# One YOCO hybrid decoder step: where the sampled sequences' new SSD states and the bias tables are made

## The chip, the cores and the metric

The kernel runs as one program on one core of a Trainium2 chip. A core has a matrix engine (TensorE, "PE" in the profile, with its weight loads listed apart as "PEld"), a vector engine (VectorE, "DVE"), an activation engine (ScalarE, "ACT"), a general engine (GpSimd, "POOL") and an engine that here only issues DMAs (SyncE, "SP"). Each works through its own list of instructions in a fixed order, and they wait for each other through semaphores. The metric is the device time of one execution in microseconds. A change is judged by the ratio of the two kernels' times in interleaved rounds on the same chip.

## What is computed

The reference is one inference step of a small two-layer decoder, for one prompt of 512 tokens and eight sampled sequences of four tokens each (544 tokens in all, width 1024). Layer one is a Mamba-2 mixer, layer two a dilated window attention; both share their weights between the prompt and the samples. Cut to what matters here:

```python
u = rmsnorm(h, g_norm) @ w_in              # 5120 columns: gate z, x, B, C (and dt)
act = silu(causal_conv(xBC))               # width 4, from state_conv for the samples
# chunked scan; for a sampled sequence there is one chunk of 4 tokens:
y      = y_diag + C @ s_in * exp(a_cs)     # reads the old state s_in
s_new  = exp(a_last) * s_in + B^T (decay_in * dt * x)      # an output, read by nothing else
h = h + rmsnorm(y * silu(z)) @ w_out       # 8 tiles of 128 columns, 16 blocks deep
kv = rmsnorm(h) @ w_kv                     # 16 tiles: 8 of values, 8 of keys
bias = rel_bias[bucket(distance)]          # per head and dilation group
... dilated attention over kv and a cache with those biases, then @ w_o, final norm
```

For the eight samples the state is 8 x 32 heads x 64 x 128 floats (8.4 MB); the old states come in as `s0`, the new ones leave as `ssmS`. The bias tables depend on the weights alone.

## The kernel before

All products are made in pairs of rounded halves: a weight tile `wraw` is split by ScalarE into a high part (`whi`, L199) and by VectorE into a low part (`wlo`, L200), activations likewise, and three matmuls (high x high, high x low, low x high) replace one. A tile of columns is done as two halves of tokens, `pa` (256) and `pb` (288). The matrix engine's instructions keep the order in which the code issues them; the other engines' orders are made by a planner that takes the earliest instruction of the program that its model holds ready, with some work raised by `high_priority` (the weight splits above all).

Buffers come from pools with a fixed number of slots for each tag. Those that matter here are `slab` (`half`, 13 slots of 128x4x544 floats, used through the whole kernel), `ss` (`pss`, five banks of PSUM), `wraw` (three raw weight tiles), and in the second stage the tag `hb` (two slots).

Four stages follow one another:

- **Stage A** (to about 368 us of the profile): the 40 tiles of `w_in` run through the matrix engine as a filler (`filler_a`), and a list of 24 units is woven in: for each of four groups `g`, four prompt chunks (`ssm_chunk`) and two quads of sampled sequences (`ssm_quad`, `q` = 0, 1; four sequences each). A quad loads its old states in two halves (`s_t`, L685), multiplies them with the output weights (`yos`, L699), splits B (`bt`, L700) and the weighted inputs (`xr`, L714) into rows of high and low parts, lets GpSimd multiply the old states in place with their decays (L723) and then, for each sequence, makes `up` on the matrix engine, adds it to the state on VectorE (L744) and stores two sequences at a time from ScalarE's DMA queue (L746). A state buffer can be loaded again only when its store has landed.
- **The out stage** (about 368 to 473 us): eight tiles of `w_out`, each 16 blocks deep, so 96 matmuls. `h1_tile` adds the residual and prepares the next activations. One step of the generator `bias_tables` runs after each tile.
- **The kv stage** (about 473 to 580 us): 16 tiles, values first, each 48 matmuls. Two steps of `bias_tables` run in each tile until it is through: 7 steps of `bvp` products, then 12 of `bs` products, each copied out by VectorE (L901, L913) and stored to DRAM. The **quarters** `bq` are the attention layer's normalized activations, their sums and differences, split into high and low parts (L1021 to L1035); they need only `h1` and the norm `rs_h`, which the second kv tile provides, and the planner puts them beside the kv tiles. They take seven slots of the slab.
- **The attention stage** (from 580 us): first products `pa<-bq`, then attention, output projection and final norm.

Of the kernel before, what the change touches and what calls it, by code (L numbers as in the profile page):

```python
# [12 lines left out]
F32 = mybir.dt.float32  # L13
# [111 lines left out]
def tile_yoco_step(  # L125
# [86 lines left out]
    def hi_lo_rows(out, src, c, rows=128):  # L212
        nc.scalar.activation(out, src, AF.Copy, scale=hls[0:rows, c + 1:c + 2])
        nc.vector.scalar_tensor_tensor(out, src, hls[0:rows, c:c + 1], f32(out), op0=ALU.mult, op1=ALU.add)
# [69 lines left out]
    sed = dram.tile([2, NH, 32], F32, name="sed")  # L284
    vnd = dram.tile([NB, TS, ATH, 128], F32, name="vnd")
    kvd = dram.tile([ATH, 128, T + SEQ], F32, name="kvd")

# [205 lines left out]
    def spread_decays():  # L493
        dx = pss("dx")
        mm(dx[:, 0:384], ones, dgs.rearrange("p a b -> p (a b)"), start=True, stop=True)
        dv = dx[:, 0:384].rearrange("p (r j h) -> p r j h", r=3, j=4)
        nc.scalar.copy(dec[:, 0:4], dv[:, 0])
        nc.scalar.copy(dec[:, 4:12].rearrange("p (j r) h -> p r j h", r=2), dv[:, 1:3])

    def tok_transposes():  # L500
# [162 lines left out]
    def ssm_quad(g, q):  # L663
# [34 lines left out]
        for j in range(4):  # L698
            mm(yo[32 * j:32 * j + 32, :], cp[:, q, j, :], s_t[j // 2][:, j % 2, :], start=True, stop=True)  # L699
        bt = wk.tile([128, 128], F32R, name="btr", bufs=1)  # L700
        hi_lo_rows(bt, cbp[:, 128:256], 0)
        cbm = wk.tile([128, 16], F32, name="cbs")
# [9 lines left out]
        with tc.high_priority():  # L712
            nc.vector.tensor_tensor(xdd, xph, bc(tok[:, 4 + q, 2, hs], HP), op=ALU.mult)
        xr = wk.tile([128, 8, HP], F32R, name="xr", bufs=1)  # L714
        hi_lo_rows(xr, xdd, 2)
        ms = wk.tile([128, 8, 16], F32, name="ms")
# [3 lines left out]
        nc.vector.tensor_tensor(ms, ms, cbm[:, None, :].to_broadcast([128, 8, 16]), op=ALU.mult)  # L720
        for j in range(4):
            sv = s_t[j // 2][:, j % 2, :].rearrange("p (a b) -> p a b", b=HP)
            nc.gpsimd.tensor_tensor(sv, sv, bc(dec[:, 4 + 4 * q + j, hs], HP), op=ALU.mult)  # L723
        yield
# [13 lines left out]

        def update(j):
            up = pss("up", (128, 8, HP))  # L740
            mm(up.rearrange("p a b -> p (a b)"), bt[32 * j:32 * j + 32, :],
               xr[32 * j:32 * j + 32].rearrange("p a b -> p (a b)"), start=True, stop=True)
            sv = s_t[j // 2][:, j % 2, :].rearrange("p (a b) -> p a b", b=HP)
            nc.vector.tensor_tensor(sv, up, sv, op=ALU.add)  # L744
            if j % 2:
                nc.scalar.dma_start(ssmS[g, :, 4 * q + j - 1:4 * q + j + 1, :], s_t[j // 2])  # L746

        for j in range(3):
            update(j)
        yield  # L750
        update(3)

# [91 lines left out]
    def h1_tile(m, pa, pb):  # L844
# [16 lines left out]
        (nc.gpsimd if m < KD - 1 else nc.vector).tensor_tensor(hss, hss, sq, op=ALU.add)  # L861

    def load_out(m):
        return [load_w(w_out[m, :, 0:8, :]), load_w(w_out[m, :, 8:16, :])]

    def bias_tables():
        rl = wk.tile([66, 384], F32, name="rl", tag="tv", bufs=2)
        relt = wk.tile([66, 384], F32R, name="relt", bufs=1)
        for i in range(2):
# [8 lines left out]
        def fetch(q):  # L878
            oh = wk.tile([66, 2 * SK], F32R, name="oh", tag="tb", bufs=2)
            if q < 2:  # L880
                oh = oh[:, 0:VN // 2]
                hot(oh, ohp[:, q * (VN // 2):(q + 1) * (VN // 2)])
            elif q < 8:
                oh = oh.rearrange("p (a b) -> p a b", a=2)
                hot(oh, ohs[:, 2 * q - 4:2 * q - 2, :])
            return oh
# [3 lines left out]
        for q in range(8):  # L890
            oh, nxt = nxt, fetch(q + 1)
            if q < 2:
                ov = wk.tile([128, VN // 2], F32, name="ov", tag="tv", bufs=2)
                c = 0
# [11 lines left out]
                continue  # L906
            bsr = wk.tile([128, 2, SK], F32, name="bsr", tag="tv", bufs=2)
            g, t = divmod(2 * q - 4, TS)
# [12 lines left out]
    for m in range(KD):  # L921
        w = nxt
        pa, pb = pj("pa"), pj("pb")
        if m == 0:
            full(pa, w, v_h, v_l, 0, HA, 0, 12)
            full(pb, w, v_h, v_l, HA, T, 0, 12)
            full(pa, w, v_h, v_l, 0, HA, 12, 15)
            full(pb, w, v_h, v_l, HA, T, 12, 15)
            ms_add(ms, ssq, inv_i, True, True)
            full(pa, w, v_h, v_l, 0, HA, 15)  # L930
            full(pb, w, v_h, v_l, HA, T, 15)
            nxt = load_out(1)
            prev = pa, pb
            continue
# [7 lines left out]
        if m + 1 < KD:  # L942
            nxt = load_out(m + 1)
        full(pb, w, v_h, v_l, HA, T)
        h1_tile(m, pa, pb)
        next(tables, 0)

# [29 lines left out]
    for i, (f, h, wi) in enumerate(order):  # L977
        w = [nxt]
        pa, pb = pj("pa"), pj("pb")
        if i == 0:  # L980
# [6 lines left out]
            full(pb, w, h_h, h_l, HA, T, 7)  # L987
            prev = pa, pb
            continue
        if i == 1:  # L990
# [12 lines left out]
        next(prev, 0)  # L1003
        next(tables, 0)
        full(pb, w, h_h, h_l, HA, T, 4)
# [3 lines left out]
        next(prev)  # L1009
        next(tables, 0)  # L1010
        if i == 8:
# [594 lines left out]
```

## Time and profile before

| what | value |
|---|---|
| median of 3 runs | 957.39 us (952.74 to 958.02) |
| the profiled execution, its own time | 955.35 us |
| its span, first to last instruction | 953.6 us |
| VectorE, ScalarE, GpSimd busy | 685.5, 477.6, 201.9 us |
| granted TensorE clock over the span | 0.983 |
| DMA, mean over the span | 177 GB/s |

The span is what the views of the profile divide up; 1.75 us of the execution lie outside it. A busy share of an engine says little by itself: the matrix engine's busy time counts a matmul from its start to the modelled end of its pipeline, so that neighbouring matmuls overlap. What one costs is read from the distance between starts.

### The profile page before, as it was taken

The page shows a single profiled execution, that of the slowest core. Times are in us where ns is not written, and L with a number is a line of the kernel's source. Part 1 is how long each engine was busy: PE and PEld are TensorE (multiplying, and loading weights), DVE is VectorE, ACT ScalarE, POOL GpSimd, SP SyncE. Part 2 cuts the span into 40 slices and gives each one's busy share as a digit, 9 for nine tenths or more (in the row PEclk, how much of TensorE's full clock was granted, in tenths as well). Part 3 has the DMA queues.
Part 4 walks back from the last instruction along what each step waited for, and adds up shares of the span by engine and source line. Part 5 has one row for each costly group of instructions (what it writes and reads, how often), then busy time and mean ns, then how long its engine had stood idle before and what let it go on. Part 6 is the DMA issues. An engine that isn't in the chain of part 4 may idle for free.

```text
span 953.6 us, 21793 instructions
## 1 busy us (share of the span) xinstructions
PE 924.2 (97%) x8645; PEld 850.3 (89%) x8645; DVE 685.5 (72%) x1435; ACT 477.6 (50%) x1057; POOL 201.9 (21%) x295
## 2 busy tenths in 40 slices
PE   7999999899999998999999999999999999999896
PEld 5999888888888888999999999988888888879896
DVE  5688998998999888555488446866667767758532
ACT  5557754755655654322254213555545555566442
POOL 3232544734634732101101000000000000000121
PEclk9999999899999999999999999999999999999898
DMA  7252355254465433536286555766877767855311
GB/s 253 91 138 93 100 200 187 84 191 151 153 206 174 172 113 111 155 101 216 97 275 215 186 176 182 261 217 214 271 236 251 258 236 215 292 194 193 113 47 48
DMA packets 75934, 168.49 MB, mean 177 GB/s; under 512 B 19446, under 2 KB 37192, under 8 KB 75320
## 3 DMA queue, kind: packets, MB, share of 16 engines
q1 hardware_dynamic: 71880, 154.91, 49.5%
q10 hardware_dynamic: 2880, 9.44, 2.5%
q0 software_dynamic: 1072, 2.74, 1.1%
q8 instruction: 68, 1.11, 0.5%
q14 instruction: 34, 0.28, 0.1%
HBM read 141.14 MB, written 25.93 MB: 175 GB/s over the span
## 4 chain that ended last, share of the span: by engine, by line
PE 87%; DVE 6%; DMA 3%; ACT 1%; POOL 1%; issue 1%; SPq 0%; DVEq 0%; ACTq 0%
PE pa L143 34%; PE pb L143 30%; PE sp L143 3%; PE so L143 3%; PE pv L143 2%; PE s L143 2%; DMA kc<-ck 1%; PE yd L143 1%; PE csp L143 1%; PE yo L143 1%; PE ptp L146 1%; PE xp L146 1%; PE w L146 1%; DVE co L529 1%; PE yos L143 1%
## 5 line engine op out<-in xcount | busy, mean ns | idle before, releaser
L199 ACT ACTIVATE whi<-wraw 128x1024 fp32r<-128x1024 f32 x72 | 76.1, 1056 | 101.5 <-PE pb L143 68.9
L200 DVE TENSOR_TENSOR wlo<-wraw,whi 128x1024 fp32r<-128x1024 f32 x71 | 90.0, 1268 | 48.1 <-ACT whi L199 47.9
L143 PE MATMUL pa<-bq,whi 128*128 128x272 f32 x512 | 103.2, 297 | 0.0
L143 PE MATMUL pa<-xh,whi 128*128 128x256 f32 (+1 forms) x320 | 92.9, 294 | 3.3 <-ACT xh L365 3.3
L143 PE MATMUL pb<-xh,whi 128*128 128x288 f32 (+1 forms) x304 | 90.4, 299 | 3.9 <-ACT cb L331 3.9
L143 PE MATMUL pb<-xl,whi 128*128 128x288 f32 (+1 forms) x304 | 91.2, 302 | 0.9 <-DVE xl L368 0.8
L143 PE MATMUL pa<-xl,whi 128*128 128x256 f32 (+1 forms) x320 | 90.7, 287 | 1.1 <-DVE xl L368 1.1
L143 PE MATMUL pb<-xh,wlo 128*128 128x288 f32 (+1 forms) x304 | 87.4, 299 | 0.0
L143 PE MATMUL pa<-xh,wlo 128*128 128x256 f32 (+1 forms) x320 | 85.0, 283 | 0.0
L143 PEld LDWEIGHTS pa<-bq,whi 128*128 128x128 f32 x512 | 81.9, 190 | 0.9
L143 PE MATMUL pb<-bq,whi 128*128 128x272 f32 x384 | 78.4, 298 | 1.0 <-DVE qpad L1091 0.7
L143 PE MATMUL pa<-bq,wlo 128*128 128x272 f32 x256 | 74.3, 290 | 0.0
L529 DVE SCALAR_TENSOR_TENSOR co<-cb,cvp,co 128x568 f32<-128x568 f32 x72 | 66.1, 919 | 1.1 <-ACT co L527 0.2
L143 PEld LDWEIGHTS pa<-xh,whi 128*128 128x128 f32 x320 | 60.8, 190 | 6.4 <-ACT xh L365 4.0
L143 PEld LDWEIGHTS pa<-xl,whi 128*128 128x128 f32 x320 | 60.6, 189 | 3.5 <-DVE xl L368 1.6
L143 PEld LDWEIGHTS pb<-xl,whi 128*128 128x128 f32 x304 | 57.8, 190 | 6.4 <-issue 4.4
L143 PEld LDWEIGHTS pb<-bq,whi 128*128 128x128 f32 x384 | 61.4, 190 | 2.3 <-DVE qpad L1091 1.4
L143 PEld LDWEIGHTS pb<-xh,whi 128*128 128x128 f32 x304 | 58.0, 191 | 5.0 <-ACT cb L331 4.1
L1333 POOL COPY lse<-mxs 128x1 f32<-128x1 f32 x16 | 4.1, 258 | 265.5 <-DVE mxs L1331 265.5
L143 PEld LDWEIGHTS pa<-xh,wlo 128*128 128x128 f32 x320 | 58.0, 188 | 1.3 <-issue 0.9
L143 PEld LDWEIGHTS pb<-xh,wlo 128*128 128x128 f32 x304 | 56.6, 190 | 2.2 <-issue 2.2
L1158 ACT ACTIVATE whi<-wraw 128x512 fp32r<-128x512 f32 x64 | 40.1, 626 | 35.9 <-PE pb L143 14.8
(378 smaller groups left out, 2788.0 us busy)
## 6 DMA issues: line engine op xcount, KB each, us to landing
wraw<-w_in SPq DMA_DIRECT2D x40, 512.0 KB
kc<-ck SPq DMA_DIRECT2D x32, 640.0 KB
vc<-cv SPq DMA_DIRECT2D x32, 640.0 KB
wraw<-wb SPq DMA_DIRECT2D x32, 512.0 KB
s<-s SPq DMA_DIRECT2D x16, 512.0 KB
m<-aed SPq DMA_DIRECT2D x16, 512.0 KB
ssmS<-s ACTq DMA_DIRECT2D x16, 512.0 KB
wraw<-w_out SPq DMA_DIRECT2D x16, 512.0 KB
```

Of the source, the lines that this page charges most:

```text
L143: pin(nc.tensor.matmul(*a, **k))
L146: pin(nc.tensor.transpose(*a))
L199: a = nc.scalar.activation(hi, raw, AF.Copy)
L200: b = lo_eng.tensor_tensor(lo, raw, f32(hi), op=ALU.subtract)
L529: nc.vector.scalar_tensor_tensor(o, cb[:, k:k + n], cvp[:, ti, k:k + 1], o, op0=ALU.mult, op1=ALU.add)
L1158: nc.scalar.activation(hi, src[p][j], AF.Copy)
L1333: nc.gpsimd.tensor_copy(lse[:, i16:i16 + 1], mx[:, 2:3])
```

## The change

In stage A a quad no longer makes its new states. It still loads the old ones and multiplies them with `cp`, but then only copies B (`bt`) and writes it and the weighted inputs (`xdd`) to a DRAM tensor `sxd`; the decays of all samples are written once to `dcd`. The new states are made in the out and kv stages by three functions. `state_load(k)` loads the four old states of quad `k` again (1 MB), with `sxd` and `dcd`; `state_prep(k)` multiplies them with the decays on GpSimd and makes the rows of high and low parts; `state_fin(k)` makes the four `up` products, adds them and stores, now from GpSimd's DMA queue. `state_step` is called twice per out tile (once in the first) and once per kv tile; quad `k` is loaded at step 3k, prepared at step 3k+2, finished at step 3k+4. So quad 0 is finished with out tile 2 and quad 7 at step 25, after kv tile 10. `bias_tables` leaves the out stage: it starts in kv tile 0, skips tile 1 and takes two steps per tile from tile 2 on, which puts its last product in tile 11. Its buffers come from the slab, as those of the states take its former room.

```diff
+    sxd = dram.tile([NG, 2, 128, 640], F32, name="sxd")
+    dcd = dram.tile([128, NG, 8, 8], F32, name="dcd")
...
+        for g in range(NG):
+            dma(dcd[:, g], dec[:, 4:12, 8 * g:8 * g + 8])
...
-        bt = wk.tile([128, 128], F32R, name="btr", bufs=1)
-        hi_lo_rows(bt, cbp[:, 128:256], 0)
+        bt = wk.tile([128, 128], F32, name="bts", bufs=2)
+        nc.scalar.copy(bt, cbp[:, 128:256])
+        dma(sxd[g, q, :, 512:640], bt)
...
-        xr = wk.tile([128, 8, HP], F32R, name="xr", bufs=1)
-        hi_lo_rows(xr, xdd, 2)
+        dma(sxd[g, q, :, 0:512], xdd.rearrange("p a b -> p (a b)"))
...
-        for j in range(4):
-            sv = s_t[j // 2][:, j % 2, :].rearrange("p (a b) -> p a b", b=HP)
-            nc.gpsimd.tensor_tensor(sv, sv, bc(dec[:, 4 + 4 * q + j, hs], HP), op=ALU.mult)
...
-        def update(j):
-            up = pss("up", (128, 8, HP))
-            mm(up.rearrange("p a b -> p (a b)"), bt[32 * j:32 * j + 32, :],
-               xr[32 * j:32 * j + 32].rearrange("p a b -> p (a b)"), start=True, stop=True)
-            sv = s_t[j // 2][:, j % 2, :].rearrange("p (a b) -> p a b", b=HP)
-            nc.vector.tensor_tensor(sv, up, sv, op=ALU.add)
-            if j % 2:
-                nc.scalar.dma_start(ssmS[g, :, 4 * q + j - 1:4 * q + j + 1, :], s_t[j // 2])
-
-        for j in range(3):
-            update(j)
         yield
-        update(3)
...
+    def state_load(k):
+        g, q = divmod(k, 2)
+        s_ = wk.tile([128, 4, 512], F32, name="sx", bufs=2)
+        dma(s_, s0[g, :, 4 * q:4 * q + 4, :])
+        sx = wk.tile([128, 640], F32, name="sxx", bufs=2)
+        dma(sx, sxd[g, q])
+        dq = wk.tile([128, 4, 8], F32, name="dq", bufs=2)
+        dma(dq, dcd[:, g, 4 * q:4 * q + 4])
+        st_q[k] = [s_, sx, dq]
+
+    def state_prep(k):
+        s_, sx, dq = st_q[k]
+        for j in range(4):
+            sv = s_[:, j, :].rearrange("p (a b) -> p a b", b=HP)
+            nc.gpsimd.tensor_tensor(sv, sv, bc(dq[:, j], HP), op=ALU.mult)
+        bt = wk.tile([128, 128], F32R, name="btr", bufs=1)
+        hi_lo_rows(bt, sx[:, 512:640], 0)
+        xr = wk.tile([128, T], F32R, name="xr", tag="hb", bufs=2)[:, 0:512]
+        hi_lo_rows(xr, sx[:, 0:512], 2)
+        st_q[k] += [bt, xr]
+
+    def state_fin(k):
+        g, q = divmod(k, 2)
+        s_, _, _, bt, xr = st_q.pop(k)
+        for j in range(4):
+            up = pss("up")
+            mm(up, bt[32 * j:32 * j + 32, :], xr[32 * j:32 * j + 32, :], start=True, stop=True)
+            nc.vector.tensor_tensor(s_[:, j, :], up, s_[:, j, :], op=ALU.add)
+            if j % 2:
+                nc.gpsimd.dma_start(ssmS[g, :, 4 * q + j - 1:4 * q + j + 1, :], s_[:, j - 1:j + 1, :])
+
+    def state_step():
+        n = st_n[0]
+        st_n[0] += 1
+        for at, f in ((4, state_fin), (2, state_prep), (0, state_load)):
+            k, r = divmod(n - at, 3)
+            if r == 0 and 0 <= k < 2 * NG:
+                f(k)
...
     def bias_tables():
-        rl = wk.tile([66, 384], F32, name="rl", tag="tv", bufs=2)
-        relt = wk.tile([66, 384], F32R, name="relt", bufs=1)
+        rl = half("rl", F32, (66, 384))
+        relt = half("relt", F32R, (66, 384))
...
-            oh = wk.tile([66, 2 * SK], F32R, name="oh", tag="tb", bufs=2)
+            if q == 8:
+                return None
+            oh = half("oh", F32R, (66, 2 * SK))
...
-                ov = wk.tile([128, VN // 2], F32, name="ov", tag="tv", bufs=2)
+                ov = half("ov", F32, (128, VN // 2))
...
-            bsr = wk.tile([128, 2, SK], F32, name="bsr", tag="tv", bufs=2)
+            bsr = half("bsr", F32, (128, 2, SK))
...
             nxt = load_out(1)
+            state_step()
             prev = pa, pb
             continue
...
             nxt = load_out(m + 1)
+        state_step()
         full(pb, w, v_h, v_l, HA, T)
         h1_tile(m, pa, pb)
-        next(tables, 0)
+        state_step()
...
             prev = pa, pb
+            next(tables)
+            state_step()
             continue
...
         next(prev, 0)
-        next(tables, 0)
+        if i > 1:
+            next(tables, 0)
         full(pb, w, h_h, h_l, HA, T, 4)
...
         next(prev)
-        next(tables, 0)
+        if i > 1:
+            next(tables, 0)
+        state_step()
```

More of the change, by code (lines that the diff above doesn't have):

```diff
@@ L861, in h1_tile @@
         (nc.gpsimd if m < KD - 1 else nc.vector).tensor_tensor(hss, hss, sq, op=ALU.add)
+    st_q = {}
+    def state_load(k):
[26 more added lines that the diff above has]
+                nc.gpsimd.dma_start(ssmS[g, :, 4 * q + j - 1:4 * q + j + 1, :], s_[:, j - 1:j + 1, :])
+    st_n = [0]
+    def state_step():
[5 more added lines that the diff above has]
+                f(k)
     def load_out(m):
@@ L882, in fetch @@
                 hot(oh, ohp[:, q * (VN // 2):(q + 1) * (VN // 2)])
-            elif q < 8:
+            else:
                 oh = oh.rearrange("p (a b) -> p a b", a=2)
```

## The prediction, made before the change was run

> **What bounds the kernel now.** I read the page first: shares of engines, then the chain that ended last.
>
> ```profile
> PE 924.2 (97%) x8645; PEld 850.3 (89%) x8645; DVE 685.5 (72%) x1435; ACT 477.6 (50%) x1057; POOL 201.9 (21%) x295
> PE 87%; DVE 6%; DMA 3%; ACT 1%; POOL 1%; issue 1%; SPq 0%; DVEq 0%; ACTq 0%
> ```
>
> The matrix engine carries 87% of the chain, so moving work of other engines can only win where it waits. Next the stretches of stage A and the start of the out stage.
>
> ```profile
> core 0: us, PE busy (x) PEld busy (x) DVE busy (x) ACT busy (x) POOL busy (x), PEclk, DMA share, GB/s
> 100.00:150.00 50.00, 49.76 (x410) 44.26 (x409) 45.03 (x73) 30.69 (x72) 22.74 (x37) 1.00 0.48 159
> 150.00:200.00 50.00, 46.06 (x366) 41.15 (x365) 48.10 (x68) 28.50 (x61) 28.91 (x38) 0.93 0.38 132
> 200.00:250.00 50.00, 48.70 (x393) 42.33 (x392) 45.63 (x71) 26.80 (x60) 28.25 (x39) 1.00 0.54 183
> 250.00:300.00 50.00, 50.00 (x425) 45.13 (x424) 45.74 (x73) 31.25 (x71) 21.12 (x34) 1.00 0.48 157
> 300.00:350.00 50.00, 50.00 (x411) 43.36 (x412) 43.58 (x74) 27.70 (x58) 29.89 (x26) 1.00 0.50 170
> 350.00:400.00 50.00, 47.14 (x363) 45.48 (x363) 38.63 (x60) 21.50 (x33) 9.14 (x8) 0.97 0.38 123
> 400.00:450.00 50.00, 50.00 (x396) 49.75 (x395) 24.71 (x37) 13.94 (x17) 6.51 (x6) 1.00 0.50 165
> ```
>
> VectorE is 87 to 96% busy in stage A and 49% in the out stage, but PE is idle for only 0.24, 3.94, 1.30, 0 and 0 us in the first five rows and for 2.86 us in the sixth. The views of waits name the three holes, and two short stretches show the granted clock behind the larger ones.
>
> ```profile
> PE pb L143 <- ACT cb L331: 3.9, 1, 3.9
> PE yos L143 <- DMA s<-s: 1.3, 1, 1.3
> PE pa L143 <- DVE wlo L200: 2.9, 1, 2.9
> 167.29:174.11 6.82, 4.81 (x21) 4.80 (x22) 6.72 (x9) 4.03 (x11) 6.59 (x9) 0.50 0.22 86
> 375.50:378.90 3.40, 3.40 (x17) 3.40 (x16) 3.37 (x4) 1.30 (x2) 1.70 (x1) 0.50 0.41 142
> ```
>
> After the 3.9 us hole the clock is 0.50 for 6.8 us, after the 2.9 us hole for 3.4 us; after the 1.3 us hole it stays 1.00. Half a clock for 6.8 and 3.4 us costs up to 3.4 and 1.7 us more. So what stage A can give back is about 3.9 + 3.4 + 1.3 + 2.9 + 1.7 = 13 us, and no more.
>
> **The change, part by part.** These are the rows of what leaves stage A.
>
> ```profile
> L143 PE MATMUL up<-xr,btr x32: 461/492/501, 117.6 to 357.9; 32*128 32x512 f32 x32
> L744 DVE TENSOR_TENSOR s<-up,s x32: 675/679/692, 121.4 to 359.3; 128x512 f32<-128x512 f32 x32
> L723 POOL TENSOR_TENSOR s<-s,dec x32: 1034/1086/2026, 102.7 to 345.5; 128x512 f32<-128x512 f32 x32
> L214 DVE SCALAR_TENSOR_TENSOR xr<-xdd,csts,xr x8: 734/739/1690, 110.2 to 350.3; 128x512 fp32r<-128x512 f32 x8
> 227.53 0.43 PE up L143 x3
> 357.87 0.49 PE L143 MATMUL up<-xr,btr 32*128 32x512 f32 x1
> 358.29 0.38 PE L143 MATMUL pa<-xh,wlo 128*128 128x256 f32 x1
> ```
>
> *PE.* The same 32 `up` products move. Three of a quad's now run side by side in 0.43 us (four use different rows of the array) and the fourth alone costs 358.29 - 357.87 = 0.42: 8 x 0.85 = 6.8 us leave. In the middle all four come together: 8 x 0.43 = 3.4, if all four find a bank. In the three finishes that stand behind a `bs` step (kv tiles 4, 7, 10) two `bs` banks and four `up` banks are one more than five; I add 0.5 each, about a `bsr` copy less the 0.24 that PE needs meanwhile (bounds 0 and 1). Net **-1.9 us** (-3.4 to 0).
>
> *VectorE, ScalarE and GpSimd in stage A* lose, per quad, 4 x 0.68 + 0.74 of VectorE and 4 x 1.09 of GpSimd, 28 and 35 us in all; B's split becomes one copy on ScalarE. That is worth only what it does to the holes. Outside them I count nothing (0 to -3): PE is busy there.
>
> *The hole at 244 us.* The chain of waits runs through a store and the reload of its buffer, and SP's own waits show that this is the rule.
>
> ```profile
> 238.23 4.62 DMA ssmS<-s
> 242.90 3.73 DMA s<-s
> SPq L685 <- DMA ssmS<-s: 49.5, 14, 8.4
> ```
>
> Without the stores the buffer is free after `yos`, a unit earlier. **-1.3 us** (0 to -3.7, the landing of the reload). In their place SP gets 16 writes of `bt` and `xdd`, which wait for ScalarE and VectorE; behind them wait the next `w_in` and `m` loads, as they did behind 49.5 us of waits for stores. I cost them at nothing, because that longer wait goes; without the cover a late `m` would hold ScalarE a few us in eight places.
>
> *The holes at 371 and 165 us.*
>
> ```profile
> 360.27:374.04 13.77, 13.77 (x17) 1.00 0.33 113
> 366.79 6.19 DVE L758 SCALAR_TENSOR_TENSOR vl<-v,gn,vh 128x544 fp32r<-128x544 f32 x4
> 372.90 1.21 DVE L200 TENSOR_TENSOR wlo<-wraw,whi 128x1024 fp32r<-128x1024 f32 x1
> 164.86 2.24 POOL L592 TENSOR_TENSOR v<-v,uz 128x544 f32<-128x544 f32 x1 [0.66 <-DVE v L584]
> 167.07 3.20 POOL L598 TENSOR_TENSOR ssq<-ssq,sq 128x544 f32<-128x544 f32 x2
> ```
>
> The first row is VectorE alone (length, busy time, clock, DMA): from 360 to 374 it has no idle moment, and `wlo` comes last. In the same queue the last quad's four adds and its `xr` stood just before, 3.5 us; without them the wait of 2.9 goes nearly whole, with its clock: **-4.2 us** (0 to -4.6). At 165 us GpSimd is the one that is late (`v`, `ssq`, then the slot that `cb` needs). Its rows there are not the states' multiplications, and an earlier VectorE spares it only the 0.66 us in the bracket; I add as much again for a PE that is itself ahead. **-1.5 us** (0 to -7.3: the hole with its clock, if the order changes).
>
> *What the middle takes.* Per quad, about every 18 us, 3.8 us of VectorE, 4.3 of GpSimd, 1 MB + 0.33 MB in and 1 MB out; the out stage's VectorE is half idle and its GpSimd busy 6.5 us in 50, so the work itself hides. The four `dcd` writes are costed at nothing: they hide under 300 us until the first read, at under 1 us of SP each by the nearest row.
>
> ```profile
> L482 SPq DMA_DIRECT2D sed<-tm x1: 632/632/632, 54.0 to 54.0; - x1
> 472.00:580.00 108.00, 108.00 (x854) 106.84 (x853) 67.35 (x129) 37.45 (x77) 5.05 (x10) 1.00 0.62 204
> 424.07 5.71 PE pa L143 x48
> 425.55 1.22 DVE L200 TENSOR_TENSOR wlo<-wraw,whi 128x1024 fp32r<-128x1024 f32 x1
> oh<-ohs POOLq DMA_DIRECT2D x12, 166.0 KB, 4.0
> ```
>
> The kv stage moves 204 GB/s at a share of 0.62; about 8 MB more in 108 us makes some 280, share 0.85. Weights are fetched three tiles ahead, so I expect no wait. The tight place is each out tile's second split: this `wlo` ends at 426.77, and PE needs it half-way through its 48 `pa`, at 426.9. An add or `xr` ahead of it costs its 0.7 us; the quads' adds come after `h1_tile` in the program, so mostly not. **+1.0 us** for the middle (0 to +5).
>
> *What goes late in turn: the quarters.* The tables' buffers now come out of the slab ahead of the quarters'. I take slots to be handed out in the program's order; nothing in the trace of before tests that. Then no quarter can be written before the last table buffer has its slot, at the end of kv tile 10; `xr` of quad 7 holds one of the two `hb` slots until there too.
>
> ```profile
> L1024 DVE SCALAR_TENSOR_TENSOR hb<-h,gn,rstd x8: 772/776/780, 484.6 to 512.5; 128x544 f32<-128x544 f32 x8
> L1035 DVE TENSOR_TENSOR bq<-hb,bq x12: 430/432/436, 487.2 to 519.7; 128x272 fp32r<-128x272 f32 x12
> 484.50:515.40 30.90, 30.90 (x68) 1.00 0.80 256
> 550.10:580.30 30.20, 12.82 (x20) 1.00 0.49 167
> L913 DVE COPY bsr<-bs 128x512 f32<-128x512 f32 x7 | 4.8, 679 | 0.0
> ```
>
> The third and fourth rows are again VectorE alone. The quarters now run from 484.6 to 519.7. The third row ends where the first part of the fourth block is done; VectorE is wholly busy in it. Its 68 instructions are 8 `hb` (0.776), 16 sums and 22 or 23 low parts (0.432), 23 us by their lengths; the other 21 are four `wlo` (1.22), the seven copies of the last row (4.8) and ten evacuations about as long as a low part, 14 us. The lengths overlap (37 against 30.9), so the quarters took 23 x 0.84, about 19. After the change they have the last five kv tiles: 30.2 us by the fourth row, in which VectorE has 12.8 us of its own. To that come quad 7's four adds and two `bsr` copies, 6 x 0.68 x 0.84 = 3.4 us; one `hb` can run early, 0.7. So 19 + 12.8 + 3.4 - 0.7 = 34.5 us against 30.2, with 0.3 for the last `bs` pair and 1.2 until the fourth block is used: about 3 us of wait at the attention stage's first products. By the hole of 2.9 us above, the clock may halve behind it: +1. **+4.0 us**. The ends are 0 (slots not in order) and 14.4: the whole 35.1 us of now, starting a tile (6.0) late, against 30.2, and 3.5 for the clock.
>
> The Trainium skill ("TensorE: Matmul & The Clock Gate", section "What's actually happening") states that the clock drops after an idle window of about 3.4 us, counted on a free-running grid. By that rule a 3 us wait would cost no clock and the term would be 3; the trace differs, since 2.9 us was enough at 371.
>
> **The sum.** -1.9 - 1.3 - 4.2 - 1.5 + 1.0 + 4.0 = -3.9. Against the profiled execution's own time, 953.6 of span and 1.75 around it: 955.35 - 3.9 = 951.4. The median of the runs is 2.0 above that execution; I add half of it and forecast **952.4 us**.
>
> **The rivals.** (1) *The quarters decide, slower.* Place: the first products after the kv stage. If the chain of `hb`, sums, casts cannot be packed tighter than now and starts with the table buffers' release, the price is 14.4: 951.4 - 4.0 + 14.4 = 961.8, with the half 963. It decides once its price passes the 8.9 us of gains less 1.0. For it speaks VectorE's full row; against it the shorter queue there. (2) *The holes of stage A stay.* GpSimd's order sets the one at 165, PE's last `z` tiles the one at 371; then 951.4 + 5.7 = 957.1, with the half 958. The full VectorE row to 374 speaks against it. (3) *The quarters are not late* (slots shared as they come free): 951.4 - 4.0 = 947.4, with the half 948.4; if GpSimd's order also spares the hole at 165 with its clock, 5.8 less, 942.6. (4) *Stores from GpSimd's queue land late*, hold the next reload and SP's queue, and a weight comes late. That queue's transfers took 4.0 us for 166 KB; one that takes the 8.4 us of SP's longest wait, at a place without cover, costs 4.4: 956.8. The Trainium skill ("SBUF — State Buffer", section "Who interferes with whom") says that such a DMA's descriptors are starved while VectorE runs certain copies, and advises the other queues; no run here shows a starved store yet.
>
> **Chances.** Forecast 0.40 (its own range 948 to 957), rival 1 0.16, rival 2 0.17, rival 3 0.20, rival 4 0.07. The range 942 to 965 takes in rivals 1 and 3 but for their tails. Over 0.5% is what a measurement of this kernel can tell. Faster: half of the forecast, rival 3, a little of the others, 0.42; slower: rival 1, 0.16; the rest 0.42.
>
> **What would show it.** `up` in fours, 0.43 us apart from the next matmul; no wait of `yos` for `s`; PE's idle at 371 under 0.5 us; `hb` starting after kv tile 10 and a PE wait of 1 to 6 us for `bq` at the first `pa<-bq`, perhaps with clock 0.50 behind it. Wrong would be: `hb` near 485 us as now, PE waits for `wlo` or weights inside the out and kv stages, or an unchanged hole at 371.

## The result, and the profile after

The changed kernel takes **962.87 us** (median of 7 runs, 960.59 to 968.35) against 956.19 us for the kernel before on the same chip (7 runs, 952.74 to 959.28). The ratio is 1.0075, 95% interval 1.0049 to 1.0102: slower by three quarters of a percent, where 952.4 us, faster, was forecast. The profiled execution took 963.51 us, of which its span is 961.7.

The page of the kernel after, engines and the chain that ended last:

```profile
PE 922.6 (96%) x8645; PEld 850.1 (88%) x8645; DVE 684.3 (71%) x1435; ACT 478.1 (50%) x1065; POOL 212.9 (22%) x311
PE 75%; DVE 11%; ACT 4%; DMA 4%; issue 3%; POOL 2%; SPq 0%; DVEq 0%; ACTq 0%
```

The work is the same to 2 us on each engine but GpSimd, which has 11 us more. But the matrix engine now carries 75% of the chain instead of 87%, and VectorE 11% instead of 6%: the engines wait for each other more. Where, is seen from the four stages. The windows begin at the first product of each stage; a row has its bounds, its length, then busy time and instructions of PE, PEld, DVE, ACT and POOL, the granted clock, the DMA share and GB/s. First the kernel before, then after:

```profile
0.00:368.09 368.09, 355.24 (x2908) 319.98 (x2909) 318.14 (x514) 216.33 (x464) 164.04 (x238) 0.99 0.47 155
368.09:472.88 104.79, 101.93 (x791) 101.00 (x789) 56.15 (x79) 31.67 (x39) 16.51 (x16) 0.98 0.40 130
472.88:580.32 107.44, 107.44 (x850) 106.28 (x848) 67.31 (x128) 37.45 (x77) 5.05 (x10) 1.00 0.63 205
580.32:888.33 308.01, 302.55 (x3679) 267.63 (x3677) 221.05 (x671) 168.51 (x433) 5.53 (x20) 0.99 0.71 233
```

```profile
0.00:355.89 355.89, 342.87 (x2877) 314.63 (x2877) 276.63 (x467) 207.94 (x455) 123.20 (x207) 1.00 0.46 144
355.89:465.82 109.93, 104.64 (x801) 101.15 (x800) 76.12 (x100) 37.49 (x51) 39.94 (x32) 0.98 0.58 200
465.82:585.50 119.68, 116.43 (x871) 111.57 (x870) 82.68 (x143) 37.62 (x76) 33.42 (x42) 0.97 0.79 278
585.50:897.68 312.18, 303.25 (x3678) 268.65 (x3677) 226.00 (x683) 171.33 (x440) 5.56 (x20) 0.99 0.69 230
```

Stage A is 12.2 us shorter, the out stage 5.1 longer, the kv stage 12.2 longer, the attention stage 4.2 longer; what follows is 1.3 shorter (65.3 to 64.0 us). That is 8.0, the difference of the spans (961.7 - 953.6 = 8.1) but for rounding. So stage A gave more than the 9.6 us that the forecast counts there (6.8 for `up`, 1.3 and 1.5 for two holes), and the two stages in the middle took back 17.4, more than all of it.

Those of PE's waits in the kernel after that bear on this (total, times, longest, in us):

```profile
PE pa L143 <- DVE wlo L200: 4.6, 3, 3.1
PE pb L143 <- ACT cb L333: 2.8, 1, 2.8
PE pa L143 <- DVE bq L1077: 2.3, 1, 2.3
PE xp L146 <- DVE cbm L633: 1.4, 1, 1.4
PE pa L143 <- ACT hh L843: 1.1, 1, 1.1
PE xp L146 <- DVE xdd L631: 1.1, 1, 1.1
PE up L143 <- ACT bsr L949: 0.9, 2, 0.4
PE up L143 <- DVE ov L936: 0.4, 1, 0.4
```

The wait of `yos` for a reload is gone. The hole at the start of the out stage (`wlo`, 3.1 us) is not. New are two of `xp` in stage A, 2.5 us together, two more waits for `wlo` inside the out stage, one for `hh` where the kv stage starts, one for `bq` where the attention stage starts, and those of `up`. What lies behind those for `wlo` and `hh` is shown by VectorE's groups in the out and kv stages (busy us, mean ns), first before, then after:

```profile
L200 DVE TENSOR_TENSOR wlo<-wraw,whi 128x1024 fp32r<-128x1024 f32 x31 | 37.9, 1221 | 30.7 <-ACT whi L199 30.7
L851 DVE TENSOR_TENSOR h<-h,xk 128x512 f32<-128x512 f32 x8 | 8.8, 1094 | 0.0
L852 DVE TENSOR_TENSOR h<-h,xk 128x32 f32<-128x32 f32 x8 | 1.5, 187 | 0.0
```

```profile
L200 DVE TENSOR_TENSOR wlo<-wraw,whi 128x1024 fp32r<-128x1024 f32 x31 | 43.6, 1406 | 15.9 <-ACT whi L199 15.8
L882 DVE TENSOR_TENSOR sx<-up,sx 128x512 f32<-128x512 f32 x32 | 20.1, 680 | 0.0
L840 DVE TENSOR_TENSOR h<-h,xk 128x512 f32<-128x512 f32 x8 | 10.3, 1286 | 0.0
L841 DVE TENSOR_TENSOR h<-h,xk 128x32 f32<-128x32 f32 x8 | 5.2, 647 | 0.0
```

The same instructions on the same shapes take longer: `wlo` 1.41 us for 1.22, the add of 32 columns of `h` 0.65 for 0.19. The adds `sx<-up,sx`, with one operand in PSUM, take 0.68 as they did in stage A. The timeline of the kernel after shows the place where it costs most. First VectorE, then GpSimd, then PE (start, length, what; the idle time before it and its releaser in brackets):

```profile
468.20 2.07 DVE L200 TENSOR_TENSOR wlo<-wraw,whi 128x1024 fp32r<-128x1024 f32 x1
470.19 1.34 DVE L841 TENSOR_TENSOR h<-h,xk 128x32 f32<-128x32 f32 x1
```

```profile
463.10 6.09 POOL L869 TENSOR_TENSOR sx<-sx,dq 128x512 f32<-128x512 f32 x4 [13.56 <-DMA sx<-s]
469.15 2.33 POOL L850 TENSOR_TENSOR hss<-hss,sqb 128x544 f32<-128x544 f32 x1
```

```profile
472.37 0.38 PE L143 MATMUL pa<-hh,whi 128*128 128x256 f32 x1 [1.11 <-ACT hh L843]
473.19 0.39 PE L143 MATMUL pa<-hl,whi 128*128 128x256 f32 x1 [0.44 <-DVE hl L844]
474.09 1.05 PE L143 MATMUL ms<-inv,hss 128*128 128x1 f32 x6 [0.41 <-DVE hss L850]
```

GpSimd waits for the load of a quad's states, multiplies them (`sx`, 6.1 us) and then adds to `hss`, which stood in its queue behind them. Beside these VectorE's `wlo` takes 2.07 us and 32 columns of `h` 1.34; `hh` and `hl` come late and PE waits three times. GpSimd's late `hss` is not itself what PE waits for: the last `hss` (L850) is VectorE's, behind `hl`. And the granted clock pays once more, by the windows of the kernel after (PE alone):

```profile
471.20:474.60 3.40, 1.44 (x9) 0.99 1.02 389
474.60:481.40 6.80, 6.80 (x27) 0.50 0.58 181
```

For 6.8 us PE runs at half clock, up to 3.4 us of delay behind 2 us of waits.

### The profile page after: what moved, and what is told of

It is laid out like the page before. It is cut to its first block, busy times and chain, and to the rows that moved or that the text cites. A ratio compares the mean times of both kernels' runs of the same rounds, so it can differ in the third digit from the quotient of the medians.

```text
span 961.7 us, 21900 instructions
## 1 busy us (share of the span) xinstructions
PE 922.6 (96%) x8645; PEld 850.1 (88%) x8645; DVE 684.3 (71%) x1435; ACT 478.1 (50%) x1065; POOL 212.9 (22%) x311
## 4 chain that ended last, share of the span: by engine, by line
PE 75%; DVE 11%; ACT 4%; DMA 4%; issue 3%; POOL 2%; SPq 0%; DVEq 0%; ACTq 0%
PE pa L143 30%; PE pb L143 25%; PE sp L143 3%; PE so L143 3%; DMA m<-aed 2%; PE pv L143 2%; DVE wlo L200 2%; PE s L143 2%; DMA kc<-ck 1%; ACT whi L199 1%; DVE vl L747 1%; DVE co L533 1%; PE ptp L146 1%; PE w L146 1%; POOL v L596 1%
## 5 line engine op out<-in xcount | busy, mean ns | idle before, releaser
L200 DVE TENSOR_TENSOR wlo<-wraw,whi 128x1024 fp32r<-128x1024 f32 x71 | 95.8, 1349 | 57.8 <-ACT whi L199 57.5
L143 PE MATMUL pb<-bq,whi 128*128 128x272 f32 x384 | 78.9, 300 | 1.5 <-DVE qpad L1133 1.2
L533 DVE SCALAR_TENSOR_TENSOR co<-cb,cvp,co 128x568 f32<-128x568 f32 x72 | 61.6, 855 | 1.4 <-ACT co L531 0.2
L869 POOL TENSOR_TENSOR sx<-sx,dq 128x512 f32<-128x512 f32 x32 | 42.2, 1346 | 85.5 <-DMA sx<-s 70.1
```

Of the source, the lines that this page charges most:

```text
L143: pin(nc.tensor.matmul(*a, **k))
L200: b = lo_eng.tensor_tensor(lo, raw, f32(hi), op=ALU.subtract)
L533: nc.vector.scalar_tensor_tensor(o, cb[:, k:k + n], cvp[:, ti, k:k + 1], o, op0=ALU.mult, op1=ALU.add)
L869: nc.gpsimd.tensor_tensor(sv, sv, bc(dq[:, j], HP), op=ALU.mult)
```

## The experiments

Ratios are to the kernel before, with 95% intervals; medians are in us. Stage lengths are from one profiled execution each.

**Leaving the multiplications out.** The first theory was the stretch: VectorE's instructions take longer beside GpSimd's.

```diff
-        for j in range(4):
-            sv = s_[:, j, :].rearrange("p (a b) -> p a b", b=HP)
-            nc.gpsimd.tensor_tensor(sv, sv, bc(dq[:, j], HP), op=ALU.mult)
```

> The changed kernel without the 32 multiplications of the old states with their decays on GpSimd (state_prep, L869), so that ssmS is made from undecayed states; all loads, rows, products, adds and stores stay. Theory: these multiplications stretch VectorE's work beside them (the add of 32 columns of h took 0.65 us on average where it took 0.19 before, wlo 1.41 for 1.22), which makes the products at 387-392 us wait 2.6 us in all and those at 471-474 us 2.5 us, with half a clock for 6.8 us behind (3.4 us). Without them: out stage about 107 us instead of 109.9, kv stage about 114 instead of 119.7, no half clock at 475, time 8 us less than the changed kernel, about 955. Rival: the waits come from the added work on VectorE itself (rows, adds) or from the added transfers; then out and kv stages change by less than 1.5 us together and the time stays at 962 to 963.

Measured: 954.20, ratio 0.998 (0.9958 to 1.0002), some 9 us less than the changed kernel. VectorE's groups in the out stage of this run:

```profile
L200 DVE TENSOR_TENSOR wlo<-wraw,whi 128x1024 fp32r<-128x1024 f32 x16 | 19.5, 1221 | 19.5 <-ACT whi L199 19.5
L841 DVE TENSOR_TENSOR h<-h,xk 128x32 f32<-128x32 f32 x7 | 1.3, 188 | 0.0
```

Both are back at their old lengths, the out stage is 108.0 us (109.9 with the multiplications) and the kv stage 112.9 (119.7), without half clock at its start. Of the added work, the rows, adds, loads and stores all stayed. So the 32 multiplications, which the prediction had costed at nothing, are what made the change slower. Without them it is level with the kernel before (the interval takes in 1), not clearly faster. Whether it is the work itself or its place on GpSimd, this run doesn't say; e16 below does.

**An earlier step of the states, against the sixth PSUM bank.**

```diff
             full(pa, w, h_h, h_l, 0, HA, 5)
+        state_step()
...
             next(tables, 0)
-        state_step()
```

> In the kv stage the step of the states is moved from the end of a tile, directly behind a pair of bs products, to between pa and pb. Theory: the four up products wait because two bs banks and four up banks are one more than the five of PSUM; the sixteen up took 4.51 us of PE in the kv stage against 1.74 in the out stage. With 48 pa ahead of them they take 1.8 us: 2.8 us less, time about 960. Rival: they wait because VectorE's queue is full at any place of the kv tile; then the adds, now ahead of wlo, make pb or the next bs wait instead, and the time is 963 or more.

Measured: 962.28, ratio 1.0054 (1.0028 to 1.008), an interval that overlaps that of the changed kernel. In the kernel after three of the quads had a gap of 0.9 us between their `up`; here these are gone, but a wait of 2.0 us for a bank that `vb` still reads has come, and the sixteen `up` of the kv stage still take 4.2 us. By itself this settles little. In the later runs with the multiplications on VectorE and this edit (e6, e12, e13) those sixteen take 1.75 us, as in the out stage.

**The tables alone.** The tables' lines of the diff (slab buffers, the start in kv tile 0, the guards of tile 1), put into the kernel before.

```diff
-        next(tables, 0)
...
+            next(tables)
...
+        if i > 1:
+            next(tables, 0)
```

> The kernel before with the tables' part of the change alone: bias_tables starts in kv tile 0, skips tile 1 and has its buffers in the slab; the states stay in stage A. Theory: the quarters wait for the tables' slab slots, so hb starts only in kv tile 11 or 12 (after 550 us), and the attention stage takes about 312 us instead of 308: about 4 us slower than before, 960. Rival: what makes the quarters late is the states' part (xr in an hb slot, adds on VectorE); then hb starts by 490 to 500 us and the time is that of before within 1 us, 956 to 957.

Measured: 956.99, ratio 1.0005 (0.9983 to 1.0026): no loss. The rows say why both theories were half right. VectorE in this run, then the windows of its kv and attention stages:

```profile
555.83 0.68 DVE L915 COPY bsr<-bs 128x512 f32<-128x512 f32 x1
557.55 0.44 DVE L1039 TENSOR_TENSOR bq<-hb,bq 128x272 fp32r<-128x272 f32 x1
586.32 0.43 DVE L1039 TENSOR_TENSOR bq<-hb,bq 128x272 fp32r<-128x272 f32 x1
```

```profile
477.49:586.09 108.60, 108.60 (x855) 107.32 (x854) 69.52 (x132) 37.46 (x77) 5.02 (x10) 1.00 0.67 217
586.09:892.99 306.90, 301.04 (x3678) 266.06 (x3676) 221.81 (x673) 168.59 (x433) 5.56 (x20) 1.00 0.71 234
```

The first two `hb` were made by 491 us, yet no quarter is written before the tables' last buffer is in use (`bsr`, from 555.83): ScalarE's first part of one comes at 556.43, VectorE's at 557.55. The slots do go in the program's order. But the last quarter is done at 586.8, just as the attention stage starts; PE doesn't wait. In the changed kernel quad 7 adds to it: its `xr` holds an `hb` slot until the last `up` at 554.5, its four adds (2.5 us) come next, and the quarters end at 594.0, with the 2.3 us wait for `bq`.

**Ending the tables earlier.** A third step of `bias_tables` in a kv tile, and room for `xr`.

```diff
-        sx = wk.tile([128, 640], F32, name="sxx", bufs=2)
+        sx = wk.tile([128, 640], F32, name="sxx", bufs=1)
...
-        xr = wk.tile([128, T], F32R, name="xr", tag="hb", bufs=2)[:, 0:512]
+        xr = wk.tile([128, 512], F32R, name="xr", bufs=1)
...
             full(pa, w, h_h, h_l, 0, HA, 5)
+        if i > 1:
+            next(tables, 0)
```

> The changed kernel with a third step of bias_tables in each kv tile from tile 2 on, so that the tables end in tile 7 instead of 11; xr gets a slot of its own instead of one of hb's two, and sxx one buffer instead of two to make room for it. Theory: quarters then start about 25 us earlier and are ready at the first products of the attention stage; attention 308 instead of 312.2 us, no half clock at 590: 4 us less than the changed kernel, about 959. Rival: the tables' products crowd PSUM and VectorE in tiles 2 to 7 and cost there what the attention stage gains (kv stage 122 to 124 us instead of 119.7): 962 to 963; with one sxx buffer a late row could also hold SP's queue.

Measured: 966.07, ratio 1.0101 (1.0069 to 1.0133). The wait for `bq` is gone, but the kv stage takes 126.7 us, more than the rival's 122 to 124. Part of it is not the crowding that the rival named: `bs` waits 3.5 us for the load of its `oh`.

**The multiplications on VectorE.** One word of the code, alone and with the earlier step.

```diff
-            nc.gpsimd.tensor_tensor(sv, sv, bc(dq[:, j], HP), op=ALU.mult)
+            nc.vector.tensor_tensor(sv, sv, bc(dq[:, j], HP), op=ALU.mult)
```

> The changed kernel with the 32 multiplications of the old states by their decays on VectorE instead of GpSimd, the same arithmetic. Theory: what cost time was GpSimd and VectorE working at once, not the amount of work; 32 x about 0.69 = 22 us more on VectorE hide in the out and kv stages (VectorE about half idle there), h's 32-column add falls back from 0.65 to 0.19 us and wlo from 1.41 to 1.22: time as without the multiplications, 954 to 956. Rival: VectorE's queue is the tight place, and 2.8 us more of it per state quad make wlo or the next activations late as before: 960 or more.

> As the run before, and with the states' step of a kv tile between pa and pb. Theory: the two costs (stretch beside GpSimd, 8 us; sixth PSUM bank, 2 us by its own run) are separate and add up: 952 to 954, faster than the kernel before by 2 to 4 us. Rival: with the multiplications on VectorE the adds come at worse moments and the earlier step gains nothing: 955 or more.

Measured: e5 972.73, ratio 1.0166 (1.0125 to 1.0207), the slowest of all; e6 961.29, ratio 1.0066 (1.0044 to 1.0088). The theory missed something: a wait. VectorE's waits and then its timeline in e5:

```profile
DVE sx L869 <- DMA sx<-s: 24.6, 6, 6.3
```

```profile
478.29 0.69 DVE L869 TENSOR_TENSOR sx<-sx,dq 128x512 f32<-128x512 f32 x1 [6.16 <-DMA sx<-s]
478.89 0.18 DVE L248 RECIPROCAL sd<-sd 128x5 f32<-128x5 f32 x1
479.56 0.68 DVE L251 TENSOR_TENSOR dg<-ident,sd 128x512 f32<-128x512 f32 x1
```

VectorE stands 6.2 us for a 1 MB load, and `dg`, for which PE waits, stands behind it. On GpSimd such a wait (70.1 us in all in the kernel after) held GpSimd and what stood behind it there.

**The hole at the start of the out stage.** `v_split` of the last group and the second weight's low part are held in the program's order, weight first.

```diff
+    for i in range(4):
+        v_split(2, i)
+    w_first = [load_w(w_out[0, :, 0:8, :])]
+    raw = fetch_w(w_out[0, :, 8:16, :])
+    with tc.high_priority():
+        w_first.append(split_w(raw, fixed=True))
+    for i in range(4):
+        v_split(3, i, hold)
```

> The changed kernel with the low part of the second weight tile of the out stage kept, in VectorE's order, ahead of the last four vl (two vl instead of four stand before it). Theory: the 2.9 us wait at the start of the out stage (pa waits for wlo, with half a clock behind it) comes from these four vl in VectorE's queue (5.1 us) and not from the state work that left; with two of them behind it the wait is about 0.5 us and the clock stays: 2.5 to 4.5 us less than the changed kernel, 958.5 to 960.5. Rival: the matrix engine comes so early that the vl themselves are then late and it waits for them instead: 962 to 963.

> Multiplications on VectorE, the states' step between pa and pb, and wlo ahead of the last vl, all three. Theory: the three costs are separate: 963 - 8 - 2 - 3 = 950, about 0.7% faster than the kernel before. Rival: one takes the other's cover and the sum is that of the best two, 953 to 955.

Measured: e7 959.97, ratio 1.0037 (1.0015 to 1.0058); the wait is 1.7 us instead of 3.1, the half clock at 362 us gone. e8, with the multiplications on VectorE, 958.43, ratio 1.0019 (0.9996 to 1.0043): the three gains don't add up while VectorE waits for loads (26.0 us for `sx` in this run).

**When, and on which engine.** e9 moves the multiplications into `state_fin` (first lines below), e10 gives them to ScalarE in a step of their own (last lines), e11 leaves them on GpSimd; all three have the earlier step and the hold of e7.

```diff
+        for j in range(4):
+            sv = s_[:, j, :].rearrange("p (a b) -> p a b", b=HP)
+            nc.vector.tensor_tensor(sv, sv, bc(dq[:, j], HP), op=ALU.mult)
...
+            for a in range(8):
+                sv = s_[:, j, HP * a:HP * a + HP]
+                nc.scalar.activation(sv, sv, AF.Copy, scale=dq[:, j, a:a + 1])
```

> As the run of all three, but VectorE multiplies the old states with their decays at the finish (state_fin, two steps later), right ahead of the up products, instead of in state_prep. Theory: the multiplications on VectorE lost because VectorE's queue stood 24.6 us waiting for the load of s (six waits, longest 6.3 us), with dg, vt and wlo behind it; two steps later the load has landed, those waits are gone, the 4 us hole before ra and the 4 us hole in vp with them: 6 to 9 us less than the run of all three, 950 to 953. Rival: the 22 us themselves in VectorE's queue delay wlo; then the out stage stays at 108 and the kv stage above 120, time 957 or more.

> As the run before, but the multiplications are made by ScalarE one step ahead of the finish, as 32 ACTIVATE of 64 columns for each quad with the decay as the scale, about 0.2 us each by the nearest row (the copy of 128 columns took 0.25): 6 to 8 us of ScalarE per quad. Theory: VectorE is the engine that counts here, ScalarE is idle two thirds of the time and shows no stretch beside the others; the time is 949 to 953. Rival: a run of 32 small instructions in ScalarE's queue stands ahead of whi or hh, and the wait for whi moves to the matrix engine: 956 or more.

> The changed kernel with the states' step between pa and pb and wlo ahead of the last vl, multiplications left on GpSimd. Theory: 963 - 2 (e2) - 3.5 (e7) = 957 to 958, so the two add up and what is left of the loss is the stretch beside GpSimd. Rival: they share a cover, 959 to 960.

Measured: e9 959.84, ratio 1.0032 (1.001 to 1.0054); e10 967.30, ratio 1.0113 (1.0091 to 1.0136); e11 959.30, ratio 1.0031 (1.0011 to 1.0051), no better than e7 alone. In e10 one ACTIVATE of 64 columns takes 0.33 us, not 0.2, so 10.7 us per quad, and PE waits 4.8 us for `whi`, as the rival had it, and 5.6 us for ScalarE's `vb` ahead of `up`. In e9 moving the lines had not moved the instructions. VectorE's timeline:

```profile
480.81 0.69 DVE L883 TENSOR_TENSOR sx<-sx,dq 128x512 f32<-128x512 f32 x1 [5.93 <-DMA sx<-s]
```

The planner takes the earliest instruction that its model holds ready, and it holds the load landed long before it is. Two steps later in the program is nearly the same place in VectorE's queue (480.81 us here, 478.29 in e5). The profiled execution of e9 was the slowest of its runs (967.29 us), so the place is read from it and not the size.

**Held behind the load.** The multiplications and the first evacuation of each tile (`h`, `vt`, `kt`) are held in the program's order, so that one can't pass the other.

```diff
+            hold(nc.vector.tensor_tensor(sv, sv, bc(dq[:, j], HP), op=ALU.mult))
...
-        nc.vector.tensor_tensor(vt[:, 0:HA], pa[:, 0:HA], rs_h[:, 0:HA], op=ALU.mult)
+        hold(nc.vector.tensor_tensor(vt[:, 0:HA], pa[:, 0:HA], rs_h[:, 0:HA], op=ALU.mult))
```

In e12 they stand in `state_fin`, in e13 in a function of their own, one step earlier. e14 is without them, and without the held evacuations, to show about what is left to gain. All three have the earlier step and the hold of e7.

> As e9, but the multiplications on VectorE are held in program order behind the evacuation of the tile before, so that the planner can't pull them ahead of the load of s. Theory: what e5, e8 and e9 paid is VectorE standing for the load of s with dg, vt and wlo behind it; held back, the wait of VectorE for s falls from 16 us (e9) to under 3, the 4.3 us hole before ra is gone, and the time is 4 to 6 us under e9: 953 to 956. Rival: the 22 us of work count wherever they stand: four multiplications and four adds in a row are 5.5 us ahead of a wlo; 958 or more.

> As e12, with the multiplications one step ahead of the adds, so that no row of eight stands in VectorE's queue (2.8 us at a time). Theory: with neither a wait for the load nor a long row, the time is that of the run without multiplications with the two other edits: 950 to 954. Rival: as for e12, 957 or more.

> The changed kernel without the multiplications of the old states (as in e1), with the states' step between pa and pb and wlo ahead of the last vl. Theory: the three costs are separate and are all there is between the changed kernel and the gain of stage A: 963 - 9 - 2 - 3.5 = 948 to 950, 0.7% faster than the kernel before. Rival: they share covers; 952 to 954, as e1 alone.

Measured: e12 951.85, ratio 0.9948 (0.9927 to 0.9969); **e13 947.40, ratio 0.9906 (0.988 to 0.9932)**; e14 946.37, ratio 0.989 (0.9871 to 0.9909). e13 computes everything and is 0.94% faster than the kernel before, 1 us above e14. In e12 and e13 VectorE's multiplications no longer wait for their load (24.6 us in e5, 16.5 in e9). The stages of e13 by the same windows as above:

```profile
0.00:358.81 358.81, 344.93 (x2876) 316.54 (x2877) 276.92 (x467) 208.56 (x455) 121.52 (x207) 0.99 0.45 143
358.81:462.89 104.08, 102.27 (x801) 99.54 (x800) 78.86 (x116) 37.60 (x51) 19.02 (x20) 1.00 0.63 217
462.89:576.04 113.15, 111.81 (x871) 108.41 (x870) 89.09 (x166) 39.82 (x82) 11.24 (x22) 1.00 0.84 289
576.04:883.99 307.95, 301.34 (x3678) 266.38 (x3677) 222.62 (x677) 168.66 (x434) 5.53 (x20) 1.00 0.71 233
```

The out and attention stages are back at the old lengths (104.8 and 308.0), though VectorE is busier in the out stage than in the kernel after (78.9 us for 76.1). So the amount of VectorE's work is not what counted. The kv stage keeps 5.7 us, of which the `up` (1.75) and the `bvp` that moved there (1.0) are half.

**What belongs to which edit.** e15 is the kernel before with the hold of e7; e16 the changed kernel with e13's multiplications and neither of the other two edits.

> The kernel before with nothing but the low part of the second out weight held ahead of the last four vl (the edit of e7). Theory: the hole at the start of the out stage is no part of the change; the same edit takes about 1.4 us of wait and the half clock from the kernel before too, 953 to 955 (ratio 0.997 to 0.999). Then of e13's 8.9 us some 2 to 3 would have been had without the change. Rival: in the kernel before the four adds of the last quad stand ahead of the same wlo, and the edit gives nothing, 956.

> The changed kernel with nothing but the multiplications moved to VectorE, held behind the evacuation and one step ahead of the adds (e13 without its two other edits). Theory: it takes the stretch away as e1 did by leaving the multiplications out: 953 to 956, within 0.3% of the kernel before, so the place of 32 multiplications decides between 0.75% slower and no loss. Rival: without the earlier step the row of adds, copies and multiplications in the kv tiles makes wlo late; 958 or more.

Measured: e15 957.52, ratio 1.002 (1.0002 to 1.0039); e16 956.38, ratio 1.0005 (0.9987 to 1.0022). The hold gives the kernel before nothing, its wait is still 2.9 us; but it also moved nothing there. VectorE's queue has the same four `vl` ahead of `wlo` as without it (from 367.95, `wlo` at 374.07), where the hold of e7 took two of them away. So e15 says only that this edit, as it is written, doesn't help the kernel before; a hold fitted to that kernel's queue was not tried. In e16 the add of 32 columns is short again:

```profile
L841 DVE TENSOR_TENSOR h<-h,xk x8: 184/194/198, 385.5 to 469.8; 128x32 f32<-128x32 f32 x8
```

The place of the 32 multiplications, with the holds that keep them there, takes the change from 0.75% slower to no difference, with intervals apart; the last percent comes with the other two edits on top of it. So it was mainly the place on GpSimd, not the work, that cost the time. What holding the evacuations does by itself was not tried.

## Why the prediction was wrong, point by point

- **What bounds it, and the cap on stage A**: right in kind. Stage A is 12.2 us shorter. Of that the `up` products make 6.9 and the wait of `yos` 1.3, as forecast; the wait at 165 us went from 3.9 to 2.8 us. In the profile after the half clock behind it (up to 3.4 us) is missing, but in e1 and e13, whose stage A is the same, it is there for 6.8 and 3.4 us: that part is chance. The two waits of `xp` take 2.5 back, which the prediction did not have. That makes at most 10.2 of the 12.2; the rest is not accounted for.
- **-1.9 for `up`**: too good. The price of the sixth bank was taken as 0.5 per finish; 0.9 was measured, at the same three finishes. The 32 `up` cost 6.25 us in the middle (1.74 and 4.51) against 6.87 in stage A: -0.6.
- **-4.2 for the hole at 371 us**: this step failed. The wait is 3.1 us where it was 2.9. The prediction saw VectorE full and took the adds of the last quad for the cause, because they stood in that queue. The chain of the kernel before through this stretch, which the prediction did not follow, has no add in it:

```profile
366.24 0.63 DVE v L592
366.87 6.11 DVE vl L758 x4
372.98 1.15 DVE wlo L200
```

  Without the adds `wlo` comes as late after the out stage's first product as with them (6.0 us before, 6.2 after), again behind four `vl`; e7 shortened the wait by putting `wlo` ahead of two of them. Rival 2 had this half right: the hole stays. But the order is not all. A `vl` takes 0.78 us as a rule, and three of these four took 1.87 to 1.89, beside three sums on GpSimd:

```profile
366.22 5.48 POOL L598 TENSOR_TENSOR ssq<-ssq,sq 128x544 f32<-128x544 f32 x3 [19.21 <-ACT sq L597]
L758 DVE SCALAR_TENSOR_TENSOR vl<-v,gn,vh x16: 772/780/1892, 340.8 to 377.2; 128x544 fp32r<-128x544 f32 x16
```

  That is 3.3 us more for the four, about as much as the hole of 2.9; in the kernel after two are stretched so, 2.2 us. So the stretch that decides the middle was already in the hole that the prediction read. How much of the hole would go with the sums elsewhere was not tried.
- **+1.0 for the middle, bounds 0 to 5**: this step failed, and it decided. "The work itself hides" was read from busy shares: VectorE half idle, GpSimd busy 6.5 us in 50. Hidden in time it was, but not beside the other engine: each multiplication stretches what VectorE does meanwhile. By the stages above, the out and kv stages grew by 5.1 + 12.2 = 17.4 us; less 6.25 for `up`, and with the `bvp` merely moved from one to the other, 11 remain, and leaving out the multiplications takes back 9 of them. The rows for it were there: the prediction itself quoted the state's multiplication at 1.09 us median and 2.03 at most on GpSimd, a spread that no equal work explains.
- **+4.0 for the quarters**: right in size (attention +4.2), right that the slots go in the program's order, wrong that this order alone makes them late: the tables alone cost nothing (e3).
- **The rivals**: rival 1 gave 963, the time that came, but by a price of the quarters that is not there. So its number is met by luck. Rival 3 (quarters not late) did not come. Of rival 4 one part came, SP's next load waits 44.8 us in all for stores from GpSimd's queue, but no weight of these stages came late: the only wait of a split for its load is 0.5 us, for `wo` at the end; and e16, with the same stores, is level with the kernel before. No rival named the stretch. The rule of the Trainium skill ("SBUF — State Buffer", section "Who interferes with whom") that would have named it stands beside the one that the prediction cited: a VectorE instruction with two SBUF inputs contends with a GpSimd instruction that reads SBUF. Here the trace agrees: `h<-h,xk` with two such inputs went from 0.19 to 0.65 us, `sx<-up,sx` with one in PSUM stayed at 0.68.
- **The marks**: `up` in fours, no wait of `yos`, `hb` behind tile 10 (all but the first, at 537 us) and a wait for `bq` with half clock behind it (3.4 us from 590.6) came as written; the unchanged hole and waits for `wlo` inside the out stage, named as marks of an error, came too.

## What to carry to other kernels

Work that moves to an idle engine is not hidden by that engine's idle time: look whose instructions run beside it, and compare the length of the same instruction with and without that neighbour. Before a hole is credited to an edit, follow the chain back through it: what stood in the same queue is not what was waited for, and an instruction of the chain may be longer there than elsewhere. And on an engine with a fixed order an instruction that waits for a load must be held behind the load's landing, since a planner that trusts its own times will pull it ahead; the same 22 us of work on VectorE instead of GpSimd cost 10 us in one place and gained 6.5 in another (e5 and e16 against the changed kernel, by the medians).

## What the runs showed of the hardware

- An add of 32 columns with both inputs in SBUF took 0.18 to 0.20 us, all eight times, in the kernel before and in e1, with no GpSimd instruction beside it. In the kernel after four of the eight met one. They took 1.03, 1.03, 1.06 and 1.34 us, and each ended 0.05 us after the GpSimd instruction that it met (which ended at 385.31, 393.70, 444.67 and 471.48). So it waited for the other's end: a short instruction behind a long one pays the most.
- Half a clock doesn't need one long hole. In the 3.4 us before the clock fell at 474.6, no wait was longer than 1.1 us; PE was busy 1.44 of 3.40 us by the row above, and the clock stayed at 0.50 for 6.8 us. The Trainium skill ("TensorE: Matmul & The Clock Gate", section "What's actually happening") speaks of an idle window of about 3.4 us; here a window only partly idle was enough.
